# VectorE block turns and DRAM exchanges for latents, rotary keys and memory queries in a two-layer hybrid encoder

## The chip, the cores and the metric

The kernel runs on one core of a Trainium2 chip (trn2). TensorE (PE) multiplies matrices, VectorE (DVE) and ScalarE (ACT) work element by element, GpSimd (POOL) and SyncE (SP) mostly issue DMAs. The metric is the device time of one launch in microseconds, the median over runs.

## What is computed

```python
for l in range(2):
    h = rmsnorm(x, pre_norm_g[l]);  z = h @ w_in[l]               # 512 tokens, 2048 wide
    q_lat, kv_lat, k_pe, gb, gc, xin, q_mem, gate = split_cols(z)
    q = rmsnorm(q_lat, q_norm_g[l]) @ w_uq[l]                     # 512 -> 8 heads x (128 + 64 rotary)
    k_nope, v = rmsnorm(kv_lat, kv_norm_g[l]) @ w_ukv[l]          # 256 -> 8 heads x (128 + 128)
    a_out = softmax attention of the 8 heads, k = [k_nope, rope(k_pe) shared]
    c_out = gb * conv3(gc * xin)
    m_out = attention of 4 heads (q_mem) over 256 memory tokens
    y = concat(a_out, c_out, m_out) * silu(gate)
    x = x + rmsnorm(y @ w_o[l], post_norm_g[l])
```

Everything is float32. A product is made of three TensorE matmuls: each operand is split into a high part (a cast to fp32r on ScalarE) and a low part (the rest, by VectorE), and high x high, high x low and low x high are added (`mm3`, lines 272 to 274; `split_to`, lines 277 and 278).

## The kernel before

**Weights.** A block of weights (128 x 1024, `wr`) comes by DMA, ScalarE casts the high half `wh` (L189), VectorE makes the low half `wl` (L190). TensorE runs 12 matmuls of 512 columns on such a block. A few blocks are in flight, so a cast waits until TensorE has left an older block. SP and POOL issue the loads in the order of the program.

**Projections.** Input and output projection use Strassen-Winograd products (P1 to P7) that are gathered in PSUM banks. The input projection has several groups of columns; the last one, "group 4", makes the gates `ga0` and `ga1` of the latent attention. Between its 28 blocks the kernel does what the attention needs: it normalises the latents (`normalise`, L983), rotates the shared key (`k_rope`), and turns both to columns.

**Turns.** Activations lie with tokens on partitions; attention needs features on partitions. In the kernel before, latents (`lat`: cq and ckv), memory queries (`qm`) and the rotary key (`krA`, `krB`) are turned by TensorE, four 128x128 transposes into a PSUM bank (`turn4`, L915, tile `tps`; `k_rope_turn`, L1021, tile `krps`), which ScalarE and VectorE then split into high and low parts. Gates go another way: VectorE turns 32x32 blocks in place (`blocks_turned`, L933), and 16 DMAs per slab of 64 KB each (`exchange`, L941) put the blocks where they belong, from SBUF to SBUF.

**Attention.** First come the rotary queries (`q_rope_steps`: `qr` on TensorE, five VectorE instructions L1067 to L1077 into `rm`, a cast `qrh`, then a trip through DRAM, `qrd` to `QR`), then four memory heads, then eight latent heads in pairs. Per head and block of 128 queries: scores `sc`, maximum `nm`, exponential `P` (L1185), scale by `rec`, turns of P into `ptp`, their split `PT`, output `o`. Queries, keys and values of the pair (`qps`, `kps`, `vps`) are computed between the memory heads, and copied out of PSUM into `Q`, `K`, `V` in two halves by ScalarE and VectorE. There are eight PSUM banks, of which each tile takes one; a tile waits for the reading of the bank's last occupant.

**Order.** Every engine runs its instructions in a fixed order that is settled when the program is built: the kernel writes steps (`put`, `add`, `defer`, `between`), and a scheduler merges them by the times that it expects. Whichever tile (a slab of 1 MB, a bank) is claimed earlier is served earlier.

**The end.** The last block of the output projection needs `T4h` and `T4l`, the split of combined weights. The residual is read back per tile of 128 tokens, in the last layer with four DMAs (`fetch`, L1372).

Of the kernel before, what the change touches and what calls it, by code (L numbers as in the profile page):

```python
# [5 lines left out]
F32 = mybir.dt.float32  # L6
# [55 lines left out]
BLOCKS = "gm", "ga0", "ga1"  # L62
# [165 lines left out]
def encoder(tc, x, xt, mem, memt, positions, columns, w_in, q_norm_g, w_uq, w_qr, kv_norm_g, w_ukv,  # L228
# [160 lines left out]
    def tables_turned():  # L389
        G["tabd"] = dram.tile([P, 2 * S], F32, name="tabd")  # L390
        for n, wide in enumerate(G.pop("wides")):
            ps = bank("tab")
            for t in range(NT):
                nc.tensor.transpose(ps[:, t * P:(t + 1) * P], wide[:, t * P:(t + 1) * P], G["ident"])
            tab = scrap("tab")
            nc.scalar.copy(tab, ps)
            nc.gpsimd.dma_start(G["tabd"][:, n * S:(n + 1) * S], tab)
# [3 lines left out]
    class Left:  # L401
# [8 lines left out]
        def split(self, name, p, src):  # L410
            t = self.ops[name, p] = slab(f"{name}{p}", F32R)
            if self.apart:
                hi, lo = (t[:, o:o + 1024].rearrange("p (t g j) -> p g t j", t=2, j=32) for o in (0, 1024))
                split_to(hi, lo, src.rearrange("p g (t j) -> p g t j", j=32))
                return
# [324 lines left out]
    def projection(l):  # L740
# [8 lines left out]
        def own(*names):  # L749
            def f():  # L750
                for n in names:
                    C[n] = slab(n).rearrange("p (g t j) -> p t g j" if n in BLOCKS else "p (t g j) -> p t g j", t=NT, j=32)
            return f
# [27 lines left out]
        def gated(*names):  # L781
            def fin(i, j, tt, ps=None):
                if names[j] is None:
                    return
                v = C[names[j]][:, 2 * i + tt]
                nc.scalar.activation(v, v if ps is None else ps, AF.Silu)

                def turn():
                    blocks_turned(v)
# [4 lines left out]
        fin_m, fin_a = gated("gm", None), gated("ga0", "ga1")  # L794
# [123 lines left out]
    def y_slab(k):  # L918
        if k not in G["ys"]:
            G["ys"][k] = slab("y").rearrange("p (j c) -> p j c", j=4)  # L920
        return G["ys"][k]
# [9 lines left out]
    def blocks_turned(v):  # L931

        nc.vector.transpose(v, v)  # L933

    def exchange(dst, src):


        for p in range(4):
            for b in range(4):
                a = src[32 * p:32 * p + 32].rearrange("i t (c b) j -> i c b (t j)", b=4)[:, :, b]  # L940
                nc.sync.dma_start(dst[32 * b:32 * b + 32, :, P * p:P * p + P], a)  # L941

    def gate_rows(k, name, C):
        def f():
            pr.until(lambda: C.get((name, "turned")) == NT)
            exchange(y_slab(k), C[name])
        return f

    def conv_turn(l, c, C):
        def f():  # L950
            ps = turn4(lambda t: C["gc"][:, t], c)
            y, w = y_slab(2)[:, c, :], G[f"cw{l}"]
# [7 lines left out]
            nc.vector.tensor_tensor(in_tiles(y), in_tiles(y), of_tiles(g), op=ALU.mult)  # L960
        return f

    def qm_turn(j, C):
        def f():
            if j == 0:
                G["Qm"] = tuple(slab(n, F32R).rearrange("p (i c) -> p i c", i=4) for n in ("QmH", "QmL"))
            ps = turn4(lambda t: C["qm"][:, t], j)
            hi, lo = G["Qm"][0][:, j, :], G["Qm"][1][:, j, :]
            nc.scalar.activation(hi, ps, AF.Copy, scale=SC_MEM)
            nc.vector.scalar_tensor_tensor(lo, ps, SC_MEM, hi.bitcast(F32), op0=ALU.mult, op1=ALU.subtract)  # L970
        return f

    def normalise(views, n, gain, by=None):
# [8 lines left out]
        def times(t, v):  # L982
            return lambda: nc.vector.scalar_tensor_tensor(v, v, r[:, t:t + 1], gain, op0=ALU.mult, op1=ALU.mult)  # L983
# [7 lines left out]

    def latents_begin(l, C):
        G["q"] = [v[:, :QR_] for v in C["lat"]]
        G["kv"] = [v[:, O_KV:O_KV + KVR] for v in C["lat"]]
        normalise(G["q"], QR_, G["grow"][0], SC_MLA)
        normalise(G["kv"], KVR, G["grow"][1])
        pr.defer(0.0, lambda: G.update(normalised=l))

    def k_rope(C):
# [7 lines left out]
        nc.vector.tensor_tensor(m1, m1, m2, op=ALU.add)  # L1007
        kr = m1.rearrange("p t s i -> p t (s i)")
        krA = scrap("krA", dt=F32R).rearrange("p (t d i) -> p t d i", t=NT, d=2)
        krB = scrap("krB", dt=F32R).rearrange("p (t d i) -> p t d i", t=NT, d=2)  # L1010
        for d in range(2):
            nc.scalar.copy(krA[:, :, d, :], kr)
            nc.vector.tensor_tensor(krB[:, :, d, :], kr, krA[:, :, d, :].bitcast(F32), op=ALU.subtract)
        G["kr"] = krA, krB

    def k_rope_turn():
        kab = slab("KAB", F32R)
        for n, src in enumerate(G["kr"]):
            ps = bank("krps", F32R)
            for t in range(NT):  # L1020
                nc.tensor.transpose(ps[:, t * P:(t + 1) * P], src[:, t].rearrange("p d i -> p (d i)"), G["identr"])  # L1021
            nc.scalar.copy(kab[:, n * S:(n + 1) * S], ps.bitcast(F32))
        G["KA"], G["KB"] = kab[:, :S], kab[:, S:2 * S]

    def latent_turn(l, tag, j):
        def f():
            if j == 0:
                pr.until(lambda: G.get("normalised") == l)
                if tag == "cq":
                    G["cq"] = tuple(slab(n, F32R).rearrange("p (k c) -> p k c", c=S) for n in ("cqH", "cqL"))  # L1030
                else:
                    both = slab("ckv", F32R).rearrange("p (s k c) -> p s k c", s=2, k=2)
                    G["ckv"] = both[:, 0], both[:, 1]
            views = G["q" if tag == "cq" else "kv"]
            ps = turn4(lambda t: views[t], j)
            H, L = G[tag]
            split_to(H[:, j, :], L[:, j, :], ps)
        return f


# [7 lines left out]
    def q_rope_steps(l, g):  # L1048
        st = {}

        def products(n):
            def f(*ops):
# [7 lines left out]
                for k in range(4):  # L1060
                    mm3(ps, (hi[:, k, n], lo[:, k, n]), (cH[:, k, :], cL[:, k, :]), k == 0, k == 3)
# [34 lines left out]
    def qkv_steps(l, pair, st):  # L1096
# [9 lines left out]
        def fq(i):  # L1106
            def g(*ch):
# [6 lines left out]
                for j in range(4):  # L1114
                    mm3(ps, (hi[:, j, :], lo[:, j, :]), (cH[:, j, :], cL[:, j, :]), j == 0, j == 3)
# [3 lines left out]
        def fk(i):  # L1119
            def g(*ch):  # L1120
# [6 lines left out]
                for j in range(2):  # L1127
                    mm3(ps, (hi[:, j, i * 256:i * 256 + P], lo[:, j, i * 256:i * 256 + P]),
                        (cH[:, j, :], cL[:, j, :]), j == 0, j == 1)
# [3 lines left out]
        def fv(b):  # L1133
            def g():
# [5 lines left out]
                for i in range(2):  # L1140
                    sl = slice((2 * b + i) * P, (2 * b + i + 1) * P)
                    for j in range(2):
                        mm3(ps[:, i * 256:(i + 1) * 256].rearrange("p (h c) -> p h c", h=2),
                            (cH[:, j, sl], cL[:, j, sl]), (hi[:, j], lo[:, j]), j == 0, j == 1)
# [6 lines left out]
    def head_iters(j, rope, src, keys, whole=False):  # L1151
# [19 lines left out]
        def score(t):  # L1171
            def g():
# [3 lines left out]
                mm3(ps, (QH[:, sl], QL[:, sl]), (KH, KL), True, rope is None)  # L1176
                if rope is not None:
                    q = G["QR"][rope // 4][:, rope % 4, sl]
                    nc.tensor.matmul(ps, q, G["KA"], start=False, stop=False)  # L1179
                    nc.tensor.matmul(ps, q, G["KB"], start=False, stop=True)  # L1180
# [21 lines left out]
        def av(b):  # L1202
            def g():
# [7 lines left out]
                if b == 1:  # L1211
                    y = G["ys"][j // 4][:, j % 4, :]
                    nc.vector.tensor_tensor(in_tiles(y), of_tiles(st["o"]), in_tiles(y), op=ALU.mult)
# [4 lines left out]
    def mla_head(h, st):  # L1218
        i = h % 2

        def src():
            Q, K, V = st["Q"], st["K"], st["V"]
            ds = slice(i * P, (i + 1) * P)
            return (Q[:, 0, i], Q[:, 1, i], K[:, 0, i], K[:, 1, i]), (lambda k: V[:, 0, k, ds], lambda k: V[:, 1, k, ds])
        return head_iters(h, h, src, S, h < HEADS - 1)

    def mem_head(i):
        def src():
            Q, K, V = G["Qm"], G["Km"], G["Vm"]
            ds = slice(i * P, (i + 1) * P)  # L1230
            return ((Q[0][:, i], Q[1][:, i], K[:, 0, i], K[:, 1, i]),
# [30 lines left out]
    def mixer(l, C, pair2, tail):  # L1262
# [3 lines left out]
        put(p0, rotate0)  # L1266
# [415 lines left out]
```

## Time and profile before

| | |
|---|---|
| median of 3 runs | 1473.79 us (1472.41 to 1474.55) |
| profiled execution | 1472.93 us, span from first to last instruction 1471.2 us |
| granted TensorE clock | 0.997 |
| PE, DVE, ACT, POOL busy | 99%, 75%, 59%, 19% |
| moved by DMA | 295.22 MB, 201 GB/s |
| group 4 of layer 0, first query matmul after it | from about 351 us; 432.24 us |

A row of a timeline is: start, duration, engine, source line, instruction, output <- input, shapes, count; in brackets the idle time before it and who ended it. In rows of groups the idle time stands at the end. A row that begins with two times and a colon is a window.

### The profile page before, as it was taken

To read this page: it belongs to the slowest core of one execution; us is meant where nothing else is said; L and a number is where in the kernel's file an instruction comes from. 1 tells how busy PE (TensorE), PEld (TensorE's weight loads), DVE (VectorE), ACT (ScalarE), POOL (GpSimd) and SP (SyncE) were. 2 spreads that over 40 slices of the span, in tenths; PEclk is the share of its full clock that TensorE was granted. 3 is DMA by queue.
4 is the path that set the end of the run, shared out by engine and by line. 5 is a ranking of instruction groups with operands and counts; after the bars stand their busy time and mean duration, and the time that the engine had idled before them with its cause. 6 is when DMAs were issued, how large, how long until landed. Compare 5 with 4: busy or idle time off the path is not lost.

```text
span 1471.2 us, 19483 instructions
## 1 busy us (share of the span) xinstructions
PE 1454.2 (99%) x7104; PEld 1239.1 (84%) x7104; DVE 1096.7 (75%) x1461; ACT 870.4 (59%) x1328; POOL 275.2 (19%) x288
## 2 busy tenths in 40 slices
PE   9999999999999999999999999999999999999996
PEld 8888888899888888888898888888988888888885
DVE  5899677957677778868879665776576777778786
ACT  7856345446458688644777434454465687775543
POOL 0032302032301100311210333020322100003021
PEclk9999999999999999999999999999999999999998
DMA  9999979697967382795987999796979655139864
GB/s 358 402 272 228 216 187 190 168 188 221 220 217 180 79 265 87 137 250 143 329 290 230 241 237 223 188 179 161 212 196 248 201 140 115 44 87 170 244 128 158
DMA packets 156672, 295.22 MB, mean 201 GB/s; under 512 B 11616, under 2 KB 46944, under 8 KB 152736
## 3 DMA queue, kind: packets, MB, share of 16 engines
q0 software_dynamic: 56768, 129.52, 43.8%
q1 hardware_dynamic: 99808, 164.45, 35.1%
q8 instruction: 56, 0.92, 0.3%
q14 instruction: 40, 0.33, 0.1%
HBM read 266.01 MB, written 21.63 MB: 196 GB/s over the span
## 4 chain that ended last, share of the span: by engine, by line
PE 88%; DMA 4%; DVE 4%; ACT 2%; issue 1%; SPq 0%; POOL 0%; POOLq 0%; DVEq 0%; ACTq 0%
PE P L273 22%; PE P L274 22%; PE P L272 22%; DMA wr<-in_w_in_dram 2%; PE ptp L1198 2%; PE o L273 1%; PE o L274 1%; PE o L272 1%; PE sc L272 1%; DVE wl L190 1%; PE sc L274 1%; PE sc L273 1%; PE tps L915 1%; PE sc L1179 1%; PE qps L272 1%
## 5 line engine op out<-in xcount | busy, mean ns | idle before, releaser
L189 ACT CAST wh<-wr 128x1024 fp32r<-128x1024 f32 (+2 forms) x436 | 445.0, 1023 | 443.0 <-PE P L274 340.2
L190 DVE TENSOR_TENSOR wl<-wr,wh 128x1024 fp32r<-128x1024 f32 (+2 forms) x436 | 515.9, 1186 | 255.2 <-ACT wh L189 251.7
L272 PE MATMUL P<-wh,S 128*128 128x512 f32 (+1 forms) x896 | 345.1, 385 | 0.0
L273 PE MATMUL P<-wl,S 128*128 128x512 f32 (+1 forms) x896 | 343.7, 384 | 0.0
L274 PE MATMUL P<-wh,S 128*128 128x512 f32 (+1 forms) x896 | 343.2, 383 | 0.0
L272 PE MATMUL P<-wh,A 128*128 128x512 f32 (+1 forms) x656 | 253.0, 386 | 0.0
L273 PE MATMUL P<-wl,A 128*128 128x512 f32 (+1 forms) x656 | 251.8, 384 | 0.6 <-DVE wl L190 0.6
L274 PE MATMUL P<-wh,A 128*128 128x512 f32 (+1 forms) x656 | 251.5, 383 | 0.0
L146 POOL DMA_DIRECT2D wr<-in_w_in_dram x132 | 158.3, 1199 | 443.6 <-DVE wl L190 279.8
L274 PEld LDWEIGHTS P<-wh,S 128*128 128x128 f32 x896 | 168.2, 188 | 30.3
L272 PEld LDWEIGHTS P<-wh,S 128*128 128x128 f32 x896 | 168.1, 188 | 29.9
L273 PEld LDWEIGHTS P<-wl,S 128*128 128x128 f32 x896 | 168.2, 188 | 29.4
L273 PEld LDWEIGHTS P<-wl,A 128*128 128x128 f32 x656 | 123.2, 188 | 22.9 <-DVE wl L190 1.4
L274 PEld LDWEIGHTS P<-wh,A 128*128 128x128 f32 x656 | 123.1, 188 | 22.2
L272 PEld LDWEIGHTS P<-wh,A 128*128 128x128 f32 x656 | 123.1, 188 | 21.8 <-ACT og L586 0.2
L146 POOL DMA_DIRECT2D wr<-in_w_o_dram x40 | 48.6, 1248 | 295.1 <-DVE wl L190 291.2
L1185 ACT ACTIVATE P<-sc,nm 128x512 f32<-128x512 f32 (+1 forms) x96 | 59.8, 623 | 28.7 <-DVE nm L1182 28.4
L1182 DVE TENSOR_REDUCE nm<-sc 128x1 f32<-128x512 f32 (+1 forms) x96 | 56.8, 595 | 14.3 <-PE sc L1180 9.1
L1188 ACT ACTIVATE P<-P,rec 128x512 f32<-128x512 f32 (+1 forms) x96 | 61.7, 659 | 8.0 <-DVE rec L1187 8.0
L1198 PE MATMUL ptp<-identr,P 128*128 128x128 f32 x320 | 46.2, 273 | 2.3 <-ACT P L1188 2.3
L178 DVE TENSOR_TENSOR wr<-wr,wr 128x1024 f32<-128x1024 f32 (+1 forms) x36 | 42.2, 1175 | 4.5 <-DMA wr<-in_w_in_dram 4.1
L1198 PEld LDWEIGHTS ptp<-identr,P 128*128 128x128 f32 x320 | 38.0, 140 | 8.8 <-ACT P L1188 3.0
(318 smaller groups left out, 2082.6 us busy)
## 6 DMA issues: line engine op xcount, KB each, us to landing
wr<-in_w_in_dram SPq DMA_DIRECT2D x128, 512.0 KB, 5.2
wr<-in_w_in_dram POOLq DMA_DIRECT2D x108, 512.0 KB, 7.4
wr<-in_w_o_dram SPq DMA_DIRECT2D x48, 512.0 KB, 6.6
wr<-in_w_o_dram POOLq DMA_DIRECT2D x40, 512.0 KB, 7.1
wr<-in_w_in_dram SPq DMA_DIRECT2D x32, 416.0 KB, 3.7
wr<-in_w_in_dram POOLq DMA_DIRECT2D x24, 416.0 KB, 5.9
wr<-in_w_mk_dram SPq DMA_DIRECT2D x15, 512.0 KB, 8.7
wr<-in_w_mv_dram SPq DMA_DIRECT2D x15, 512.0 KB, 10.6
```

Source lines behind the costliest of these rows:

```text
L146: engine.dma_start(dst, src, **kw)
L178: nc.vector.tensor_tensor(tiles[a], tiles[a], tiles[b], op=ALU.add)
L189: pin(nc.scalar.copy(hi[:, h], src[:, h]))
L190: pin(nc.vector.tensor_tensor(lo[:, h], src[:, h], hi[:, h].bitcast(F32), op=ALU.subtract))
L272: nc.tensor.matmul(ps, ah, bh, start=first, stop=False, **kw)
L273: nc.tensor.matmul(ps, ah, bl, start=False, stop=False, **kw)
L274: nc.tensor.matmul(ps, al, bh, start=False, stop=last, **kw)
L915: nc.tensor.transpose(ps[:, t * P:(t + 1) * P], v[:, 4 * j:4 * j + 4].rearrange("p g j -> p (g j)") if len(v.shape) == 3 else v[:, j * P:( ...
L1182: nc.vector.tensor_reduce(nmax, ps, axis=AX.X, op=ALU.max, negate=True)
L1185: nc.scalar.activation(pt, ps, AF.Exp, bias=nmax, accum_out=tot)
L1188: nc.scalar.activation(pt, pt, AF.Copy, scale=rec)
L1198: nc.tensor.transpose(ps[:, k * P:(k + 1) * P], pt[:, k * P:(k + 1) * P], G["ident"])
```

## The change

1. Memory queries, normalised q and kv latents and the rotated key are turned by VectorE in 32x32 blocks, as the gates are, in slabs `ql` (two instructions), `kvl` (one; it holds kv latents and key) and `qm`. The 48 turns per layer on TensorE go. Weight columns are put in block order beforehand.
2. The blocks are exchanged through DRAM: one send per slab (two for `kvl`) with `sent`, then four fetches in runs of 2 KB with `fetched`. The gates, which had 16 DMAs per slab, use the same way. The high and low parts of the latents are made from the fetched slab in SBUF (`latents_parts`, `qm_parts`), in instructions of 1024 or 768 columns.
3. Operands keep the block layout (`spots`, `by_tokens`): matmuls read runs of 128 tokens. Operands of the output projection in layer 0 are split in two instructions instead of one.
4. The residual in the last layer is fetched with one DMA per tile instead of four.
5. Sends and fetches stand at new places among the steps.

```diff
-    def blocks_turned(v):
-        nc.vector.transpose(v, v)
-    def exchange(dst, src):
-        for p in range(4):
-            for b in range(4):
-                a = src[32 * p:32 * p + 32].rearrange("i t (c b) j -> i c b (t j)", b=4)[:, :, b]
-                nc.sync.dma_start(dst[32 * b:32 * b + 32, :, P * p:P * p + P], a)
+    def sent(key, *parts):
+        n = sum(t.shape[-1] for t in parts) // 4
+        d = G["sent", key] = dram.tile([4, P, n], F32, name=nm(f"sent{key}"))
+        o = 0
+        for t in parts:
+            w = t.shape[-1] // 4
+            nc.sync.dma_start(d[:, :, o:o + w].rearrange("b q k -> q b k"), t.rearrange("q (b k) -> q b k", b=4))
+            o += w
+    def fetched(key, name, c=4):
+        t, d = slab(name), G.pop(("sent", key))
+        for b in range(4):
+            nc.sync.dma_start(t[32 * b:32 * b + 32, :512 * c].rearrange("i (p k) -> i p k", p=4),
+                              d[b].rearrange("(p i) k -> i p k", p=4))
+        return t
...
+    def latents_parts():
+        t, hi = G.pop("cqw"), slab("cqH", F32R)
+        lo = t.bitcast(F32R)
+        for h in (slice(0, 1024), slice(1024, D)):
+            pr.defer(1.2, lambda h=h: split_to(hi[:, h], lo[:, h], t[:, h]))
...
-        put(p0, rotate0)
+        put(p0)
+        add(sent_rows("ga1", C))
+        put(rotate0)
...
-        between.setdefault(2, []).append((gate_rows(0, "ga0", C), []))
+        between.setdefault(2, []).append((sent_rows("ga0", C), []))
+        between.setdefault(4, []).append((gate_back(0, "ga0"), []))
         between.setdefault(6, []).append((fetch0, []))
-        between.setdefault(12, []).append((gate_rows(1, "ga1", C), []))
+        between.setdefault(9, []).append((gate_back(1, "ga1"), []))
...
-                if last:
-                    for i in range(NT):
-                        nc.gpsimd.dma_start(x[32 * i:32 * i + 32], G["src"][P * i + 32 * t:P * i + 32 * t + 32, :])
-                else:
-                    nc.gpsimd.dma_start(x, G["src"][t * P:(t + 1) * P, :])
+                nc.gpsimd.dma_start(x, G["src"].rearrange("(t p j) c -> p t j c", p=4, j=32)[t] if last else
+                                    G["src"][t * P:(t + 1) * P, :])
...
-        put(g4[8:13])
-        add(gate_rows(3, "gm", C))
-        put(g4[13:16])
-        lat = [latent_turn(l, "cq", j) for j in range(4)] + [latent_turn(l, "ckv", j) for j in range(2)] + [k_rope_turn]
-        more = [(f, []) for f in lat + [qm_turn(j, C) for j in range(4)]]
-        put(weave(g4[16:], more, 2, 2)[:-2])
+        put(g4[8:14])
+        add(lambda l=l: latents_sent(l))
+        put(g4[14:17])
+        add(latents_back)
+        add(lambda: G.update(qmw=fetched("qm", "QmL")))
+        put(g4[17:20])
+        add(latents_parts)
+        add(qm_parts)
+        put(g4[20:24])
+        add(gate_back(3, "gm"))
```

The order of TensorE's matmuls stays as it was, without the turns. On the other engines instructions move, at three places above all.

VectorE in group 4, where the products of ga1's first half are read out of their banks (`P`), before:

```order
L190 TENSOR_TENSOR wl_3456<-wr_3162,wh_3455 128x1024
L278 TENSOR_TENSOR cqL_3440<-tps_3441,cqH_3439 128x512
L278 TENSOR_TENSOR cqL_3440<-tps_3448,cqH_3439 128x512
L543 TENSOR_TENSOR ga_128_3030<-ga_127_3029,P_131_3041 128x16x32
L543 TENSOR_TENSOR ga_128_3030<-ga_127_3029,P_132_3042 128x16x32
L190 TENSOR_TENSOR wl_3474<-wr_3200,wh_3473 128x1024
```

and after:

```order
L190 TENSOR_TENSOR wl_3455<-wr_3176,wh_3454 128x1024
L190 TENSOR_TENSOR wl_3473<-wr_3214,wh_3472 128x1024
L190 TENSOR_TENSOR wl_3500<-wr_3267,wh_3499 128x1024
L547 TENSOR_TENSOR ga_134_3042<-ga_133_3041,P_137_3053 128x16x32
L547 TENSOR_TENSOR ga_134_3042<-ga_133_3041,P_138_3054 128x16x32
```

The two readings of P moved behind two more weight splits (wr_3200 and wr_3214 are the same block).

ScalarE in the memory heads, where the values V leave their first bank, before:

```order
L277 CAST PT_3962<-ptp_4014 128x2x128
L1188 ACTIVATE P_3974<-P_3974,rec_3977 128x256
L1185 ACTIVATE P_4008,tot_4009<-sc_4002,nm_4006 128x256
L277 CAST V_4031<-vps_4032 128x512
L1188 ACTIVATE P_4008<-P_4008,rec_4011 128x256
L1185 ACTIVATE P_4025,tot_4026<-sc_4019,nm_4023 128x256
```

and after:

```order
L1207 ACTIVATE P_4098,tot_4099<-sc_4092,nm_4096 128x256
L1210 ACTIVATE P_4098<-P_4098,rec_4101 128x256
L189 CAST wh_4106<-wr_3590 128x1024
L189 CAST wh_4110<-wr_3610 128x1024
L277 CAST V_3975<-vps_3976 128x512
```

Before, it was the eleventh exponential that stood ahead of V; now it is the sixteenth and last (P_4098) with two weight casts. The casts of K and the VectorE rotation `rm` moved back in the same way, and in the last latent heads of a layer the second pair of `PTl` on VectorE stands behind the split of an operand S, which stood behind it.

ScalarE at the end of the kernel, around T4h, before:

```order
L189 CAST wh_12764<-B_1184_12445 128x1024
L586 COPY og_11668<-P_1182_12415 128x512
L1346 ACTIVATE junk,ssqo_1123_11669<-og_11668 128x512
L586 COPY og_11679<-P_1183_12416 128x512
L189 CAST T4h_12768<-wr_12256 128x1024
L189 CAST T4h_12768<-wr_12274 128x1024
```

and after:

```order
L189 CAST wh_12634<-B_1180_12327 128x1024
L189 CAST T4h_12638<-wr_12138 128x1024
L189 CAST T4h_12638<-wr_12156 128x1024
L189 CAST T4h_12658<-wr_12174 128x1024
L189 CAST T4h_12658<-wr_12192 128x1024
L590 COPY og_11550<-P_1178_12297 128x512
```

The four casts moved ahead of the copies of the products.

More of the change, by code (lines that the diff above doesn't have):

```diff
@@ L61 @@
 RAW, PIECES, SLABS = 8, 4, 19
[L62 removed]
+BLOCKS = "gm", "qm", "ga0", "ga1"
 class Unit:
@@ L412, in split @@
             if self.apart:
[L413 to L414 removed]
+                if src.shape[-1] == P:
+                    split_to(t[:, :1024], t[:, 1024:], src.rearrange("q g k -> q (g k)"))
+                    return
+                hi, lo = (t[:, o:o + 1024].rearrange("q (t c p j) -> q t p c j", t=2, p=4, j=32) for o in (0, 1024))
+                for i in range(2):
+                    split_to(hi[:, i], lo[:, i], src[:, :, 32 * i:32 * i + 32].rearrange("q (p c) j -> q p c j", p=4))
                 return
@@ L916, in turn4, with spots, by_tokens @@
         return ps
[L918 to L921, printed above, removed]
+    def spots(t, c=4):
+        return t.rearrange("q (p c k) -> q c p k", p=4, c=c)
+    def by_tokens(a):
+        return a.rearrange("q (p k) -> q p k", p=4)
     def of_tiles(a):
@@ L1006, in k_rope @@
                 nc.vector.tensor_tensor(m2[:, t, s, :], kp[:, 1 - s, :], G["sin2"][:, t, s, :], op=ALU.mult)
[L1007 to L1030, printed above, removed]
-                else:
[L1032 to L1038, printed above, removed]
+        kr = G["kvl"][:, 1024:1536].rearrange("p (g t j) -> p t g j", t=NT, j=32)
@@ new lines, in k_rope, with latents_sent @@
+        nc.vector.tensor_tensor(kr[:, :, :2], m1, m2, op=ALU.add)
+        nc.scalar.copy(kr[:, :, 2:], kr[:, :, :2])
+        for h in (slice(0, 1024), slice(1024, D)):
+            pr.defer(1.2, lambda h=h: nc.vector.transpose(G["ql"][:, h], G["ql"][:, h]))
+        pr.defer(1.8, lambda: nc.vector.transpose(G["kvl"][:, :1536], G["kvl"][:, :1536]))
+        pr.defer(0.0, lambda: G.update(normalised=l))
+    def latents_sent(l):
+        pr.until(lambda: G.get("normalised") == l)
+        sent("ql", G.pop("ql"))
+        kv = G.pop("kvl")
+        sent("kvl", kv[:, :1024], kv[:, 1024:1536])
@@ new lines, in latents_back, with there @@
+    def latents_back():
+        G["cqw"], G["ckw"] = fetched("ql", "cqL"), fetched("kvl", "ckvL", 3)
+    def latents_parts():
+        t, hi = G.pop("cqw"), slab("cqH", F32R)
+        lo = t.bitcast(F32R)
+        for h in (slice(0, 1024), slice(1024, D)):
+            pr.defer(1.2, lambda h=h: split_to(hi[:, h], lo[:, h], t[:, h]))
+        kt, khi = G.pop("ckw"), slab("ckvH", F32R)
+        klo = kt.bitcast(F32R)
+        for h in (slice(0, 768), slice(768, 1536)):
+            pr.defer(1.0, lambda h=h: split_to(khi[:, h], klo[:, h], kt[:, h]))
+        def there():
+            G["cq"] = spots(hi), spots(lo)
+            kh, kl = (spots(a[:, :1536], 3) for a in (khi, klo))
+            G["ckv"] = kh[:, :2], kl[:, :2]
+            G["KA"], G["KB"] = kh[:, 2], kl[:, 2]
+            G["latents"] = True
+        pr.defer(0.0, there)
@@ L1470, in use @@
             G["ys"] = {}
+            for n in ("cq", "ckv", "Qm"):
+                G.pop(n, None)
         ms = mem_steps(l)
@@ L1589, in encoder @@
         put(g4[2:8])
-        add(lambda C=C: k_rope(C))
-        put(g4[8:13])
-        add(gate_rows(3, "gm", C))
-        put(g4[13:16])
-        lat = [latent_turn(l, "cq", j) for j in range(4)] + [latent_turn(l, "ckv", j) for j in range(2)] + [k_rope_turn]
-        more = [(f, []) for f in lat + [qm_turn(j, C) for j in range(4)]]
-        put(weave(g4[16:], more, 2, 2)[:-2])
+        add(lambda l=l, C=C: k_rope(l, C))
+        put(g4[8:14])
[8 more added lines that the diff above has]
+        add(gate_back(3, "gm"))
+        put(g4[24:26])
         add(mem_fetch)
-        put(weave(g4[16:], more, 2, 2)[-2:])
-        G["left"] = Y = Left(False, l + 1 < depth)
+        put(g4[26:])
+        add(lambda: pr.until(lambda: "Qm" in G and "cq" in G))
+        G["left"] = Y = Left(False, True)
         g0, g1, gains, fetch = out_proj(l)
```

106 lines of the change are left out of this document (59 added, 47 removed).

## The prediction

> **What bounds the kernel now.** I read the page's busy shares, then the waits of TensorE (us in all, times, longest), then the timelines of the stages that the change touches:
>
> ```profile
> PE 1454.2 (99%) x7104; PEld 1239.1 (84%) x7104; DVE 1096.7 (75%) x1461; ACT 870.4 (59%) x1328; POOL 275.2 (19%) x288
> ...
> PE ptp L1198 <- ACT P L1188: 2.3, 2, 1.1
> ...
> 432.24 0.48 PE L272 MATMUL qr<-cqH,wh 128*128 128x512 f32 x1
> 433.02 0.39 PE L272 MATMUL qr<-cqH,wh 128*128 128x512 f32 x1
> 437.56 0.39 PE L274 MATMUL qr<-cqH,wl 128*128 128x512 f32 x1
> ```
>
> TensorE is nearly never idle, so whatever leaves its queue is time won, and every new pause of it is time lost. Its largest wait inside the layers is 1.1 us for one late probability, once a layer. Matmuls of 512 columns start 0.227 us apart (20 of them from 433.02 to 437.56), a weight block of 12 takes 2.7.
>
> All sums stand against the profiled execution, 1472.93 us (span 1471.2). The median, 1473.79, lies 0.86 above it; I add that at the end.
>
> **The turns that leave TensorE.** The instructions (duration, count, both layers), and two places in the chain of work that ended last (krB's eight turns read like krA's):
>
> ```profile
> L915 PE MATMUL tps<-identr,lat x48: 270/272/273, 399.9 to 1139.4; 128*128 128x128 f32 x48
> L915 PE MATMUL tps<-identr,qm x32: 272/272/297, 419.6 to 1158.3; 128*128 128x128 f32 x32
> L1021 PE MATMUL krps<-identr,krA x8: 223/240/251, 418.9 to 1145.2; 128*128 128x128 f32 x8
> ...
> 400.08 0.87 PE tps L915 x8
> 419.08 0.64 PE krps L1021 x8
> ```
>
> They are pipelined: eight take 0.87 on the path, 0.109 each, not 0.27; a key turn 0.08. 80 x 0.109 + 16 x 0.08 = -10.0 us, all of it on the path. The matmuls that use the turned operands stay as many; they read them in runs of 128 instead of 512 tokens, which I cost at nothing.
>
> **The turns that VectorE gets**, in the last group of the input projection (latents done, gates being made):
>
> ```profile
> L933 DVE STREAM_TRANSPOSE ga<-ga 128x512 f32<-128x512 f32 x7 | 4.8, 700 | 0.2 <-ACT ga L786 0.2
> ...
> 340.00:371.00 31.00, 31.00 (x148) 27.41 (x147) 25.97 (x41) 20.52 (x38) 7.93 (x10) 1.00 0.73 196
> ...
> 369.98 0.75 DVE L1013 TENSOR_TENSOR krB<-kpm,krA 128x256 fp32r<-128x256 f32 x2
> 371.32 1.23 DVE L190 TENSOR_TENSOR wl<-wr,wh 128x1024 fp32r<-128x1024 f32 x1 [0.59 <-ACT wh L189]
> 374.05 1.22 DVE L190 TENSOR_TENSOR wl<-wr,wh 128x1024 fp32r<-128x1024 f32 x1 [1.50 <-ACT wh L189]
> ```
>
> Two of 1024 and one of 1536 columns, 0.7 per 512: some 4.7 us, less 0.8 for the key's low halves that go. They fall where VectorE has just caught up (it first idles at 371.32, then 1.5 per block). Ends: 0, all inside the lead of the low weight halves, and 3.9, none; with one or two blocks of lead I take 1.5 a layer, +3.0. The memory queries' turns fall in the group before, on VectorE too; their two sends stand ahead of four weight loads on SP's queue: 0 to 2 us, taken as 0.
>
> [...]
>
> **The round trip through DRAM.** Before, nothing waited for it; now the split latents do:
>
> ```profile
> 378.39 19.74 SPq L941 DMA_DIRECT2D y<-gm  x16
> 401.07 1.07 ACT L277 CAST cqH<-tps 128x512 fp32r<-128x512 f32 x2
> ...
> QR<-qrd POOLq DMA_DIRECT2D x16, 256.0 KB, 7.1
> ...
> Vmd<-Vm POOLq DMA_DIRECT2D x2, 1024.0 KB, 8.3
> ...
> qrd<-rm POOLq DMA_DIRECT2D x4, 512.0 KB, 5.5
> ```
>
> SP is done with the weight loads at 378.4. A 1 MB send lands some 8 us after, 388; the fetches, four issues each, land by about 399 to 403. The new cast of cq stands at about 403.5 on ScalarE: nothing to pay, margin 1 to 5 us. If it is gone, casts and splits of weights queue behind the late cast and TensorE stops 1:1. The gates' fetches are needed only by the latent heads, over 20 us later. The rotated queries, which already go through DRAM (the rows of QR and qrd), start that trip 14 us later by place 2 below, at t 24: 5.5, four issues, 7.1 make 39, needed at 41; 0, with a margin of 2. The residual's single DMA per tile lands as one instead of four; nothing waits for it, 0.
>
> **Three places where the static order holds TensorE.** In order, per layer:
>
> (1) The last group's product banks. Before, VectorE emptied them right after two splits of cq; now after two more weight splits:
>
> ```profile
> 402.34 1.28 DVE L278 TENSOR_TENSOR cqL<-tps,cqH 128x512 fp32r<-128x512 f32 x2
> 403.54 1.27 DVE L543 TENSOR_TENSOR ga<-ga,P 128x512 f32<-128x512 f32 x2
> 403.72 1.05 ACT L189 CAST wh<-wr 128x1024 fp32r<-128x1024 f32 x1 [1.59 <-PE P L274]
> ```
>
> The last of those splits needs a cast that ScalarE can only start when TensorE has left the block before (the 1.59 wait). So TensorE comes to the banks, and then run: 0.2 release, cast 1.05, split 1.15, emptying 0.68: 3.2 idle a layer, +6.4.
>
> (2) The memory heads (first query matmul at 432.24 = t 0):
>
> ```profile
> 445.97 0.44 PE L1198 MATMUL ptp<-identr,P 128*128 128x128 f32 x2 [1.13 <-ACT P L1188]
> 461.77 0.36 PE L272 MATMUL sc<-Km,QmH 128*128 128x256 f32 x1
> 465.10 0.48 PE L272 MATMUL sc<-K,Q 128*128 128x512 f32 x1
> ...
> 435.45 1.23 DVE L1067 TENSOR_TENSOR rm<-qr,tab 128x1024 f32<-128x1024 f32 x1
> 451.42 0.68 DVE L278 TENSOR_TENSOR K<-kps,K 128x512 fp32r<-128x512 f32 x1
> 457.63 0.68 DVE L278 TENSOR_TENSOR V<-vps,V 128x512 fp32r<-128x512 f32 x1
> ...
> 441.19 1.05 ACT L277 CAST qrh<-rm 128x1024 fp32r<-128x1024 f32 x1
> 465.67 1.99 ACT L189 CAST wh<-wr 128x1024 fp32r<-128x1024 f32 x2
> ```
>
> Before: the rotation (five instructions, 3.6 us, from 435.45) ahead of the softmax, K after the sixth exponential, V after the eleventh. Now the rotation stands after the fourth PT split, K in a block with four PT casts after the twelfth exponential, V after the sixteenth and two weight casts. I walked the new order by hand with the durations of these rows. Softmax starts earlier (first turn of P at t 12.4, was 13.7, its 1.13 pause gone). Then VectorE rotates from t 17.4 to 21.4, ScalarE waits 1.9 for it; the K block, VectorE's 0.7 at its end, frees the bank of the 13th score at 28.4, 3.5 later than before; the last memory score comes at 33.7 (was 29.5). V: last scale ends 36.0, two weight casts 2.0, V cast 0.5, and on VectorE both low halves to 39.5, V 0.7: first latent score at 40.2, where it was 32.9. With 0.3 at the output behind it 7.7; in layer 1 one scale stands ahead of the second K cast, 8.5: +16.2.
>
> (3) The last latent heads, where out-projection operands are split between them:
>
> ```profile
> 582.32 1.27 DVE L278 TENSOR_TENSOR PTl<-ptp,PTh 128x512 fp32r<-128x512 f32 x2
> 583.46 0.39 PE L272 MATMUL o<-PTh,V 128*128 128x512 f32 x1
> 584.29 1.23 DVE L278 TENSOR_TENSOR S<-y,S 128x1024 fp32r<-128x1024 f32 x1
> ```
>
> The second pair of PTl now follows two maxima, the first pair and two half splits of S: six instructions of 0.6 behind a probability, 3.3 after the output needs them, and 1.0 at the score ahead: about 4.1 a layer, +8.2.
>
> **The tail gains.** ScalarE's T4h casts now precede the copies that waited for the last products:
>
> ```profile
> 1443.95 0.59 ACT L586 COPY og<-P 128x512 f32<-128x512 f32 x1 [5.75 <-PE P L274]
> 1446.39 3.88 ACT L189 CAST T4h<-wr 128x1024 fp32r<-128x1024 f32 x4
> 1447.49 0.80 PE L272 MATMUL P<-T4h,A 128*128 128x512 f32 x1 [2.22 <-ACT T4h L189]
> 1449.73 0.80 PE L273 MATMUL P<-T4l,A 128*128 128x512 f32 x1 [1.45 <-DVE T4l L190]
> 1462.30 0.39 PE L274 MATMUL P<-T4h,A 128*128 128x512 f32 x1
> 1447.20:1454.10 6.90, 5.17 (x11) 3.76 (x12) 6.90 (x7) 3.07 (x4) 0.00 (x0) 0.51 0.21 83
> ```
>
> (The last row is a window: span, busy time and count of each engine, granted clock, DMA share and GB/s.) Casts done by about 1442 and low halves by 1445 let T4's 48 matmuls start at 1445.1 and end at 1456.0 instead of 1462.5: pauses 3.7 and half clock gone, -6.7.
>
> **The clock.** That row shows that a pause of 2.2 us is followed by granted clock 0.5; the 1.13 pause at 445.97 was not. The new order has six pauses of about 3 us (place 1, before the first latent score, place 3, twice). After the second pause there the slow stretch was 4.4 us, 2.2 lost; ends 0 and 2.2 each; I take 1.0, +6: these pauses are longer than the one that did it, but stand alone, where the tail has two in a row.
>
> **Sum.** 1472.93 - 10.0 + 3.0 + 6.4 + 16.2 + 8.2 - 6.7 + 6 = 1496.0, and 0.9 to the median: 1496.9. My walk counts every wait in full; engines a little ahead of it make it less, so I say 1495.
>
> **The rivals.**
> - *The waits don't bind (faster).* The order is the same, but TensorE has other banks and work in hand when one is late. Then only -10.0, -6.7 and +3.0 count: 1460. It decides if places 1 to 3 cost under 14 us in all instead of 31. For it: in the old order all such waits came to 1.1 us a layer. Against: TensorE's queue is in order, and that 1.1 was one probability late by as much. 0.14.
> - *One or two of the places cost nothing,* by slack that I don't see: 1472 to 1487. 0.16, a quarter of it within 0.2%.
> - *The clock stays full:* 1491. For it: the 1.13 pause passed. Against: the tail. 0.18.
> - *The clock falls at all six pauses, 2.2 each:* 1504. For it: the tail's row, with a shorter pause. 0.08. [...]
> - *The round trip is late* past its margin, 3 to 5 us a layer: above 1504. 0.05.
>
> **How the numbers follow.** My forecast, places and clock as counted, 1491 to 1501, has 0.39. A measurement of this kernel can tell 0.2% (2.9 us) from no change. Faster: the first rival, 0.14. Same: the quarter of the second, 0.04. Slower: the rest, 0.82. Without the first rival and the late round trip (0.19) the cases reach from about 1472 to 1504: that is the range.
>
> **What would show it.** Right: no turns of lat and qm on TensorE; TensorE idle 3 us each time at the second pass of the last group, at the first score from K, and at the last output of a layer; no wait for T4h at the end. Wrong: those waits under 1 us, or a DMA named ahead of cq's cast on ScalarE. What would make the forecast wrong is above all place 2, half of the loss.

## The result, and the profile after

The changed kernel takes 1535.01 us (median of 4, 1524.37 to 1538.15), the kernel before in the same runs 1473.57: a ratio of 1.0405, interval 1.0378 to 1.0431. Five further runs of it gave 1531.98 (1.0403, 1.0385 to 1.0422). I had said 1495, with 1472 to 1504 as the range. The direction was right, the forecast loss about a third of the measured one.

The profiled execution took 1538.15 (span 1536.3, granted clock 0.979). First its busy line from the page, then the waits of TensorE (us in all, times, longest):

```profile
PE 1465.4 (95%) x7008; PEld 1241.2 (81%) x7008; DVE 1108.2 (72%) x1477; ACT 873.2 (57%) x1328; POOL 270.4 (18%) x276
```

```profile
PE P L272 <- DVE ga L547: 13.6, 2, 6.8
PE P L272 <- ACT wh L189: 11.5, 2, 6.3
PE o L273 <- DVE PTl L278: 6.1, 2, 3.1
PE sc L272 <- DVE V L278: 5.4, 2, 2.7
PE P L273 <- DVE wl L190: 5.3, 6, 1.3
```

Third and fourth row are places 3 and 2 of the forecast, each near the 3 us of idle time that it named (3.1 and 2.7). The first is place 1, but 6.8 long instead of 3.2, and the second wasn't in the forecast at all. Both are in group 4. For T4h TensorE waits no more, as forecast. The timeline of ScalarE and TensorE there, in layer 0, says who is late:

```profile
410.79 1.04 ACT L189 CAST wh<-wr 128x1024 fp32r<-128x1024 f32 x1 [5.36 <-DMA wr<-in_w_in_dram]
415.32 1.99 ACT L277 CAST cqH<-cqL 128x1024 fp32r<-128x1024 f32 x2 [3.48 <-DMA cqL<-sentql]
426.20 0.83 ACT L277 CAST ckvH<-ckvL 128x768 fp32r<-128x768 f32 x1 [8.89 <-DMA ckvL<-sentkvl]
...
413.84 0.77 PE L272 MATMUL P<-wh,S 128*128 128x512 f32 x1 [6.78 <-DVE ga L547]
429.07 0.80 PE L272 MATMUL P<-wh,S 128*128 128x512 f32 x1 [5.19 <-ACT wh L189]
```

Each of the two pauses of TensorE ends behind a ScalarE cast that waited for a DMA: the first behind a weight load 5.36 late, the second behind the fetch of ckv 8.89 late. The weight cast behind that one in ScalarE's queue (427.99) is what TensorE then waits for. The cast of cq in the second row waited 3.48 too; that is the sign of being wrong that the prediction had named, a DMA ahead of cq's cast. The DMA rows (KB each, median us from issue to landing) show the trip, and the same two kinds of transfer for the gates:

```profile
sentql<-ql SPq DMA_DIRECT2D x2, 1024.0 KB, 14.9
cqL<-sentql SPq DMA_DIRECT2D x8, 256.0 KB, 17.2
ckvL<-sentkvl SPq DMA_DIRECT2D x8, 192.0 KB, 15.7
sentkvl<-kvl SPq DMA_DIRECT2D x2, 512.0 KB, 21.0
sentkvl<-kvl SPq DMA_DIRECT2D x2, 256.0 KB, 26.6
...
sentga<-ga SPq DMA_DIRECT2D x4, 1024.0 KB, 6.3
y<-sentga SPq DMA_DIRECT2D x16, 256.0 KB, 9.9
```

The same 1 MB send takes 6.3 in the attention and 14.9 in group 4, and the two sends of kvl, issued right behind, take 21.0 and 26.6. A warning stood in the trace of before (first two windows, of its group 4: span, busy times, clock, DMA share, GB/s):

```profile
380.00:390.00 10.00, 10.00 (x46) 8.29 (x45) 6.66 (x8) 5.94 (x8) 4.34 (x4) 1.00 1.10 230
390.00:400.00 10.00, 10.00 (x46) 8.23 (x45) 4.90 (x4) 3.49 (x4) 3.41 (x4) 1.00 1.12 205
62.80:72.50 9.70, 9.70 (x47) 7.95 (x45) 5.89 (x10) 7.17 (x10) 2.03 (x3) 1.00 1.02 412
786.80:793.80 7.00, 7.00 (x32) 5.79 (x32) 5.87 (x10) 5.06 (x8) 1.07 (x2) 1.00 0.97 330
```

The DMA engines were already full in group 4 (share above 1.0). TensorE waited for none of them there, so it cost nothing; the change put such a wait in. But the share by itself would not have given the price. The last two rows are the times of the two `Vmd` sends, from whose median of 8.3 the prediction took its 8 us: they landed in 9.7 and 7.0 at a share of about 1 as well.

For all comparisons I cut each profiled execution at marks of TensorE's timeline, each the start of a matmul, and add the two layers: group 4 (last matmul of 416 columns to first query product `qr`), memory heads (to the first latent score from `K,Q`), latent heads (to the last `o` made from `PTh`), and the end (first T4 matmul to the end of the span). All in us:

| kernel | group 4 | memory heads | latent heads | end | span |
|---|---|---|---|---|---|
| before | 163.0 | 65.8 | 241.8 | 23.7 | 1471.2 |
| changed | 190.4 | 84.0 | 259.1 | 24.9 | 1536.3 |
| changed, again | 183.4 | 82.5 | 259.6 | 24.1 | 1529.7 |
| resid4 | 172.7 | 83.7 | 260.6 | 23.8 | 1518.4 |
| b_resid1 | 163.0 | 65.6 | 241.8 | 27.1 | 1474.1 |
| no_trip | 154.9 | 69.2 | 251.4 | 25.9 | 1481.7 |
| no_accum | 165.5 | 83.9 | 259.2 | 21.8 | 1506.5 |
| act_send | 175.2 | 78.1 | 262.6 | 26.1 | 1520.4 |
| tab24 | 175.8 | 74.6 | 253.3 | 24.6 | 1508.8 |
| stack | 173.4 | 74.8 | 242.1 | 19.4 | 1486.2 |
| lat_pe | 159.6 | 75.1 | 243.7 | 19.3 | 1475.0 |
| lat_t24 | 159.6 | 76.5 | 241.6 | 19.9 | 1475.2 |
| b_sp4 | 163.0 | 65.7 | 241.8 | 19.5 | 1464.9 |

The change's 65.1 us of span are 27.4 in group 4, 18.2 and 17.3 in the heads, 1.2 at the end, and 1.0 elsewhere. Group 4 of the changed kernel differs by up to 18 us between executions with the same order up to there (190.4, 183.4, and 172.7 in resid4); in the three executions of the kernel before in the table (before, b_resid1, b_sp4) it is 163.0 each time.

### The profile page after: what moved, and what is told of

Same layout as the page of the kernel before. It is cut to its first block, busy times and chain, and to the rows that moved or that the text cites. A ratio compares the mean times of both kernels' runs of the same rounds, so it can differ in the third digit from the quotient of the medians.

```text
span 1536.3 us, 19277 instructions
## 1 busy us (share of the span) xinstructions
PE 1465.4 (95%) x7008; PEld 1241.2 (81%) x7008; DVE 1108.2 (72%) x1477; ACT 873.2 (57%) x1328; POOL 270.4 (18%) x276
## 3 DMA queue, kind: packets, MB, share of 16 engines
q0 software_dynamic: 58112, 129.52, 41.5%
## 4 chain that ended last, share of the span: by engine, by line
PE 74%; DMA 12%; DVE 6%; issue 4%; ACT 2%; POOL 1%; SPq 1%; POOLq 0%; DVEq 0%; ACTq 0%
PE P L273 18%; PE P L274 17%; PE P L272 17%; DMA sentkvl<-kvl 3%; DVE wl L190 2%; DMA wr<-in_w_in_dram 2%; PE ptp L1220 2%; DMA ckvL<-sentkvl 2%; DMA xr<-xs 1%; PE o L273 1%; PE o L274 1%; PE o L272 1%; PE sc L272 1%; PE sc L274 1%; PE sc L273 1%
## 5 line engine op out<-in xcount | busy, mean ns | idle before, releaser
L273 PE MATMUL P<-wl,S 128*128 128x512 f32 (+1 forms) x896 | 347.2, 387 | 5.1 <-DVE wl L190 5.1
L272 PEld LDWEIGHTS P<-wh,S 128*128 128x128 f32 x896 | 169.9, 190 | 57.6 <-issue 14.4
L274 PEld LDWEIGHTS P<-wh,S 128*128 128x128 f32 x896 | 169.9, 190 | 30.6
L273 PEld LDWEIGHTS P<-wl,A 128*128 128x128 f32 x656 | 123.3, 188 | 22.8 <-DVE wl L190 1.2
```

What stands on the lines that cost most here:

```text
L272: nc.tensor.matmul(ps, ah, bh, start=first, stop=False, **kw)
L273: nc.tensor.matmul(ps, ah, bl, start=False, stop=False, **kw)
L274: nc.tensor.matmul(ps, al, bh, start=False, stop=last, **kw)
```

## Experiments

**The trip taken out (no_trip).** Rivals: the late trip, or the casts and splits that now stand between those of the weights.

```diff
-        sent("ql", G.pop("ql"))
-        kv = G.pop("kvl")
-        sent("kvl", kv[:, :1024], kv[:, 1024:1536])
...
-        G["cqw"], G["ckw"] = fetched("ql", "cqL"), fetched("kvl", "ckvL", 3)
+        G["cqw"], G["ckw"] = G.pop("ql"), G.pop("kvl")
```

> The changed kernel without the trip of latents and rotary key through DRAM: no sends and fetches of ql and kvl, the parts are made straight from the turned slabs, so blocks aren't exchanged and the attention works on wrongly placed tokens. Theory (the trip and the weight loads that it delays on saturated DMA engines stop TensorE in group 4): the two pauses there shrink to the 3 us of the bank emptying, some 14 us a layer, 28 in all with the half clock behind them: 1505 to 1510. Rival (the casts and splits that stand between those of the weights are the cause, whatever they wait for): 6 us less at most, 1529 or more.

Measured: 1485.22 (1482.08 to 1488.68), 1.0078 of before (1.0058 to 1.0099): 50 us less, more than the theory said. Group 4 falls to 154.9, which is 8.1 below before: nearly the whole 10.0 of the turns is there, so VectorE's turns and place 1 cost at most 1.9 in this order. But place 1 itself is another: without the trip VectorE empties the banks after one weight split fewer, at 402.83, and TensorE doesn't pause there. The memory heads fell too (69.2), because the scheduler starts the rotation ahead of the first maximum again. So this run changes the trip and places 1 and 2 together, and no_accum and tab24 separate them.

**The jam (no_accum).** By the jam I mean that many transfers share full DMA engines and each lands late. Here the order of instructions is the same on every engine, and only the weight loads are lighter (GpSimd's queue takes 28.2% of the 16 engines' span instead of 41.5%).

```diff
-            move(nc.gpsimd, tiles[u.key], 0, u.more, accum_op=ALU.add)
+            move(nc.gpsimd, tiles[u.key], 0, u.more)
```

> The changed kernel with the second half of each paired weight load written plainly instead of added in the DMA (it leaves out that sum, so the weights are others); the order of instructions on every engine is the same. Theory (the DMA engines are jammed in group 4, most of all by these adding loads, whose 2 KB packets take some 0.2 us against 0.09 for plain ones, and the trip of the latents shares them): sends and fetches land in 7 to 11 us instead of 15 to 21, group 4 takes 79 to 83 us a layer instead of 94 to 96, in all 24 to 32 us less: 1503 to 1511. Rival (the trip is slow by its own form, runs of 2 KB and their issue): 5 us less at most.

Measured: 1508.81 (1506.07 to 1514.04), 1.0238 (1.0220 to 1.0257). Its DMA rows:

```profile
sentql<-ql SPq DMA_DIRECT2D x2, 1024.0 KB, 9.6
cqL<-sentql SPq DMA_DIRECT2D x8, 256.0 KB, 9.5
...
sentkvl<-kvl SPq DMA_DIRECT2D x2, 512.0 KB, 10.2
```

Sends and the fetch of cq land in some 10 us, near what I had counted on, and group 4 falls by 24.9, to 165.5; the heads do not move (83.9 and 259.2 against 84.0 and 259.1). So the jam costs 24.9 of the first execution's group 4, 17.9 of the second's (183.4), and 23 to 26 by the medians. The DMA share from 380 to 430 is still 1.02 to 1.15, against 1.08 to 1.15 in the changed kernel, so the share doesn't tell the two runs apart. ScalarE still waited 5.2 for ckv in layer 0, where TensorE no longer paused behind it. What is left in group 4 is place 1, but for one wait of 1.5 in layer 1 (the last row is a window, with the granted clock after the busy times):

```profile
406.88 1.28 DVE L547 TENSOR_TENSOR ga<-ga,P 128x512 f32<-128x512 f32 x2
...
407.71 0.76 PE L272 MATMUL P<-wh,S 128*128 128x512 f32 x1 [3.08 <-ACT cqH L277]
408.27 0.63 PE L273 MATMUL P<-wl,S 128*128 128x512 f32 x1
408.70 0.63 PE L274 MATMUL P<-wh,S 128*128 128x512 f32 x1
...
413.39 0.41 PE L273 MATMUL P<-wl,S 128*128 128x512 f32 x1
413.64 0.39 PE L274 MATMUL P<-wh,S 128*128 128x512 f32 x1
...
407.70:413.40 5.70, 5.69 (x14) 4.44 (x15) 2.79 (x4) 0.57 (x1) 0.00 (x0) 0.50 1.24 333
```

3.08 against the 3.2 of my walk. (The releaser named, the cast of cq, is the event nearest in time; in the changed kernel the same matmul started at 413.84, before that cast began at 415.32. The first half of the emptying by VectorE, in the first row, ends at about 407.6.) Then the matmuls start 0.43 apart instead of 0.227, at a granted clock of 0.50: 14 steps in 5.93 instead of 3.18, so the half clock costs another 2.75 a pause. Twice 5.8 is 11.7, and no_trip, where place 1 is gone as well, has a group 4 that is 10.6 shorter than this one: that leaves next to nothing for the trip itself with the lighter loads.

**Earlier sends (act_send).**

```diff
-        sent("ql", G.pop("ql"))
+        sent("ql", G.pop("ql"), by=nc.scalar)
...
-        sent("kvl", kv[:, :1024], kv[:, 1024:1536])
+        sent("kvl", kv[:, :1024], kv[:, 1024:1536], by=nc.scalar)
```

> The changed kernel with the sends of latents and rotary key issued by ScalarE instead of SyncE, so that they leave when the turns are done (372 and 376 us) and not when SyncE is through with its weight loads (380 to 384). Theory A (what counts is when the sends leave): the trip ends 6 to 7 us earlier, and group 4 loses that much a layer, 10 to 14 us in all: 1521 to 1525. Theory B (it is the jam that counts, and an earlier start only stands longer in it, while ScalarE pays for the issues): within 5 us of 1533.

Measured: 1519.94 (1516.65 to 1522.16), 1.0308 (1.0293 to 1.0323), 1 us below the range of theory A. The sends leave at 372.9 and 376.9 and 377.7, the fetch of cq is issued at 381.95 instead of 394.29. Group 4 is 15 shorter than in the first execution of the changed kernel, 8 than in the second, but 2.5 longer than in resid4. The run doesn't show theory A's cause, though: the edit moved VectorE's order too. It now empties the banks of place 1 one weight split earlier (at 404.82), and the pause there is gone, which was worth up to 11.7 in no_accum. How much of the gain is the earlier start and how much is place 1 stays open. The trip still isn't covered: fetches of 16.6, and waits of up to 4.5.

**Place 2 (tab24).** The scheduler had put the rotation late because its table arrives through a weight buffer that is claimed late.

```diff
         put(g4[24:26])
+        add(tables_fetch)
...
-        add(tables_fetch)
         (p0, rotate0, fetch0), (p1, rotate1, fetch1) = (q_rope_steps(l, g) for g in range(2))
```

> The changed kernel with the fetch of the rotation tables four weight blocks earlier, before the last two of group 4: it moves the five rotation instructions of VectorE back ahead of the first softmax maximum, as they stood in the kernel before. Theory (place 2 of the forecast: rotation, K and V late by the static order cost 8.8 and 9.5 us between first query product and first latent score): 14 to 18 us less, 1517 to 1521. Rival (that stretch is long because of half clock and of DMAs that run late out of group 4, not by the place of the rotation): 5 us less at most, 1530 or more.

Measured: 1509.43 (1507.55 to 1510.59), 1.0241 (1.0226 to 1.0256), 26 less. The stretch of the theory, the memory heads, is 9.4 shorter, so of its 18.2 about half; the latent heads are 5.8 shorter; the rest lies in group 4, which scatters by as much, and can't be credited to the table. The total lies below the theory's 1517 to 1521 because it holds these two as well. Where the first latent score waited 2.7 for V, nothing waits, but a new pause has come:

```profile
487.82 0.50 PE L272 MATMUL sc<-K,Q 128*128 128x512 f32 x1 [2.73 <-DVE V L278]
```

```profile
PE ptp L1220 <- ACT P L1210: 7.0, 2, 3.5
PE o L273 <- DVE PTl L278: 6.1, 2, 3.1
```

The first row is from the changed kernel, the other two are waits of tab24: the first probability is now 3.5 late in each layer, since VectorE rotates before it takes the maxima. Half of place 2 is thus traded, not won.

**The residual (resid4, b_resid1, after_again, b_sp4, b_sp1).** In resid4 the changed kernel gets the old four DMAs back, in b_resid1 the kernel before gets the single one (its diff is shown; that of resid4 is the reverse):

```diff
-                    for i in range(NT):
-                        nc.gpsimd.dma_start(x[32 * i:32 * i + 32], G["src"][P * i + 32 * t:P * i + 32 * t + 32, :])
+                nc.gpsimd.dma_start(x, G["src"].rearrange("(t p j) c -> p t j c", p=4, j=32)[t] if last else
+                                    G["src"][t * P:(t + 1) * P, :])
```

> The changed kernel with the residual of the last layer fetched by four DMAs of 32 tokens per tile again, nothing else. Theory (the single DMA of 1 MB is slow, 22.8 us, and holds back the last weight load behind it on GpSimd's queue and the last residual add): about 7 us less, 1528, with T4h waiting for no DMA and the end 9 us after the last matmul instead of 14. Rival (the whole end is late because of what comes before it, and the fetch only shares in that): within 1.5 us of the changed kernel's 1535.

> The kernel before with the residual of the last layer in one DMA per tile, nothing else. Theory (one DMA is itself slow): 5 to 8 us more than before, 1479 to 1482, since the last residual tile is then waited for. Rival (it is slow only beside the other transfers of the changed kernel, or nothing waits for it, as I forecast): within 1 us of 1473.6.

> The changed kernel once more, unaltered, as the measure of its own scatter: its first four runs lie between 1524 and 1538, those with only the residual fetch put back between 1520 and 1541, and the profiled executions differ in group 4 (94.2 and 96.2 against 85.4 and 87.3). Theory (arrival times on jammed DMA engines differ from run to run): again a spread of over 10 us and a median between 1524 and 1536, which leaves the residual fetch worth under 3 us. Rival (the residual fetch is worth the 9 us between the two medians): 1533 to 1537, spread under 8.

resid4: 1526.26, 1520.18 to 1540.7, 1.0389 (1.0333 to 1.0445). after_again: 1531.98, 1531.21 to 1538.6: the median that the theory named, but a spread of 7 and not of over 10. The medians differ by 6 to 9, but the end by only 1.1 (24.9 to 23.8), so the rest is group 4's scatter; by totals alone this pair decides nothing. b_resid1: 1474.39, ratio 1.0000 (0.9991 to 1.0010): its rival. But "nothing waits" isn't why. In b_resid1 the T4h casts move ahead and T4 takes 10.6 instead of 14.8; from the last T4 matmul to the end it takes 16.5 instead of 8.9, with this wait of VectorE and this landing:

```profile
DVE xr L1396 <- DMA xr<-xs: 8.5, 1, 8.5
```

```profile
xr<-xs POOLq DMA_DIRECT2D x4, 1024.0 KB, 23.2
```

A gain and a loss of the same edit cancel. Before, 256 KB landed in 7.9. In the changed kernel the slow DMA shows as follows (GpSimd, ScalarE, VectorE):

```profile
1502.56 1.22 POOL L146 DMA_DIRECT2D wr<-in_w_o_dram  x1 [17.24 <-DVE ms L282]
```

```profile
1509.82 1.06 ACT L189 CAST T4h<-wr 128x1024 fp32r<-128x1024 f32 x1 [4.53 <-DMA wr<-in_w_o_dram]
```

```profile
1526.26 1.28 DVE L1422 SCALAR_TENSOR_TENSOR xr<-og,r,xr 128x1024 f32<-128x1024 f32 x1 [6.69 <-DMA xr<-xs]
```

GpSimd idles 17 us between the residual's DMA and its last weight load. (The releaser named there is only the event nearest in time; the load does not wait for `ms` in the program. What held it, the records don't show. The load issued before it, at 1483.37 between two residual DMAs, landed only 20.7 later.) So the last T4h cast is 4.5 late, and the last residual add 6.7. Keeping the early casts without the slow DMA is one edit, in the kernel before:

```diff
-                        nc.gpsimd.dma_start(x[32 * i:32 * i + 32], G["src"][P * i + 32 * t:P * i + 32 * t + 32, :])
+                        nc.sync.dma_start(x[32 * i:32 * i + 32], G["src"][P * i + 32 * t:P * i + 32 * t + 32, :])
```

> The kernel before with the four DMAs of each residual tile issued by SyncE, which has nothing to do then, instead of GpSimd; it also puts the T4h casts of ScalarE ahead of the last product copies, as in the changed kernel. Theory (the early casts are worth the two pauses and the half clock in front of the last block, 4.3 us as the run with a single residual DMA showed, and that run gave it back because its transfer was late by as much): 4 to 6.5 us less than before, 1467 to 1470. Rival (the end waits for the residual or for VectorE whatever TensorE does): within 1 us of before.

Measured: 1467.20 (1465.85 to 1468.71), 0.9952 of before (0.9940 to 0.9965). It beats both kernels. T4 starts at 1445.49 without a pause, and 256 KB land in 5.0. From the last `o` to the first T4 matmul it takes 133.0 instead of 135.4, and the end 4.2 less: 6.6, where the forecast's tail said 6.7.

The single DMA by SyncE instead of GpSimd, in the kernel before:

> The kernel before with the residual in one DMA per tile, issued by SyncE. Theory A (a single DMA of four blocks of 32 rows keeps only half of the DMA engines busy, on any queue): it lands in 18 to 24 us, and the end waits for it, 1472 to 1476. [...]

Measured: 1487.05, one run, longer than theory A said; the trace gives no landing time for these DMAs. A window and a wait of it:

```profile
1430.00:1440.00 10.00, 7.71 (x20) 5.81 (x21) 6.64 (x6) 4.98 (x6) 0.62 (x1) 0.66 0.36 103
```

```profile
PE P L272 <- ACT wh L189: 8.9, 2, 5.5
```

Counted from the DMA records, mostly 3 or 4 packets of 8 KB are in flight here, for some 50 us (the DMA share is 0.25 to 0.27 of 16 engines from 1396 to 1410); in b_resid1 mostly 4 or 8 (4 while only its first tile is under way), and in b_sp4 mostly 16. The end is 19.7, shorter than before; the whole loss lies between the last `o` and the first T4 matmul, 149.9 instead of 135.4. The four weight loads that GpSimd issues beside the residual land in 13.4 to 14.0 instead of the 6.0 to 8.7 of b_sp4, ScalarE's T4h casts wait up to 9.1 for them, and the weight cast that TensorE waits for stands behind those casts. That these loads share the few busy engines fits the counts, but the records name no engine.

**Everything together (stack).** Edits of tab24, act_send and b_sp4, and, for place 3:

```diff
-        last_pair = {0: [(sums(0), []), g0[0][0]], 1: [g0[0][1]], 2: [g0[0][2]], 3: [g0[0][3]],
+        last_pair = {0: [g0[0][0]], 1: [g0[0][1]], 2: [(sums(0), []), g0[0][2]], 3: [g0[0][3]],
```

> The changed kernel with four edits together: tables fetched early (as above), sends of latents and key by ScalarE (as above), the sums for the output projection two steps later in the last pair of heads (so that the second pair of PTl no longer stands behind the splits of S, place 3 of the forecast), and the residual in four DMAs per tile by SyncE. Theory (the losses are separate and add up: about 25 for the tables' place, 13 for the sends, 10 to 12 for place 3, of which 3.1 a layer is the pause and 2 to 3 half clock, 6 for the end): 1478 to 1486, with no wait for PTl. Rival (the pauses stand in for one another: what is saved at one is waited for at the next): 1495 or more.

Measured: 1487.98 (1487.71 to 1489.46), 1.0101 (1.0086 to 1.0117), 2 us above the theory's range and far from the rival. The latent heads are back at 242.1, with no wait for PTl; against tab24 that is 11.2, 5.6 a layer, most of it place 3 with its half clock. In the changed kernel the place read:

```profile
612.07 0.80 PE L273 MATMUL o<-PTl,V 128*128 128x512 f32 x1 [3.08 <-DVE PTl L278]
612.66 0.63 PE L274 MATMUL o<-PTh,V 128*128 128x512 f32 x1
613.09 0.63 PE L272 MATMUL o<-PTh,V 128*128 128x512 f32 x1
```

What remains above before is 10.4 in group 4, where the trip has eaten the turns' gain as well (place 1's pause is gone here too, as in act_send, but TensorE still waits 9.2 for weight casts), and 9.0 in the memory heads.

**Latents by TensorE again (lat_pe, lat_t24).** Turns, splits and keys as before; memory queries and gates stay on the new way, the residual as in b_sp4. In these two the latents' tokens stand in their natural order while the other operands have block order, so the outputs are others; number and size of the latents' instructions are those of the kernel before. lat_t24 adds the edit for place 3 and the early tables.

> The changed kernel with latents and rotary key turned by TensorE and split from its banks as before, so that only memory queries and gates go through DRAM, and with the residual in four DMAs per tile by SyncE. Theory (all that the exchange costs outside place 3 comes from the trip of the latents): group 4 back at 81.5 or below, the stretch to the first latent score at 33 to 36, place 3 still there, the end 6 to 7 shorter: 1473.8 - 3.5 (turns of memory queries) + 10 (place 3) - 7 + 0 to 6 for the memory heads' order = 1473 to 1479. Rival (memory queries and gates through DRAM jam the engines as well): group 4 over 85 and 1485 or more.

> The same as the run before (latents and key by TensorE, residual by SyncE) with the sums of the output projection two steps later and the tables fetched early. Theory (place 3 and the heads' order are then gone and the turns of the memory queries are won): 1463 to 1468, at or below the 1467.2 of the kernel before with the residual by SyncE. Rival (gates and memory queries in 2 KB runs give nothing back, or another wait takes their place): 1470 or more.

lat_pe: 1476.72, 1.0025 (1.0016 to 1.0034), in the theory's range. Group 4 is at 159.6, 3.4 below before: that is the 32 turns of the memory queries (32 x 0.109 = 3.5), and gates and memory queries through DRAM cost nothing more there. The total is partly luck: I had expected place 3 to stay, and its order was gone already (243.7), while the memory heads are 9.3 longer than before instead of up to 6. lat_t24: 1474.81, 1.0011 (1.0002 to 1.0020), the rival. Its memory heads take 10.7 more than before:

```profile
PE ptp L1248 <- ACT P L1238: 8.9, 2, 4.5
```

```profile
439.78 1.22 DVE L1118 TENSOR_TENSOR rm<-qr,tab 128x1024 f32<-128x1024 f32 x1
```

The rotation begins 7.6 after the first query product (432.14; before, 3.2 after it), since it now stands behind the low half of one more weight block, and the first probability comes 4.5 late. Another wait has taken the place of the one removed.

## Why the forecast was wrong, point by point

- **Round trip at nothing: the step that failed.** I took 8 us for a 1 MB send from two sends of another stage, gave the sends of kvl no time of their own, and held a late trip at a chance of 0.05 and 3 to 5 us a layer. In group 4 the send of cq took 14.9 and those of kvl 21.0 and 26.6, beside the adding weight loads. That cost 24.9 us in the first execution, 17.9 in the second, as the run with the same order and lighter loads shows, and its scatter makes most of that of the kernel.
- **Residual at nothing: failed too.** The single DMA took 22.8 us, and VectorE waited 6.7 for it at the end. The tail's gain of 6.7 was real (6.6 in b_sp4), but the early casts and the slow transfer came from the same edit. At the end the changed kernel gained nothing: 0.3 less before T4 and 1.2 more after. Why one DMA keeps fewer packets of 8 KB in flight (mostly 4 or 8 in the changed kernel) than four (mostly 16 in the kernel before), no run shows.
- **Place 1: right.** 3.08 against 3.2.
- **Place 2: right in size.** The memory heads are 8.7 and 9.5 longer, against 7.7 and 8.5, with the wait for V at the first latent score that the walk gave. The rotated queries' trip, which I had put at 0 with a margin of 2, was late once: TensorE waited 1.6 for QR in layer 1, and 4.0 in resid4.
- **Place 3: right.** 3.08 and 0.66 a layer against 3.3 and 1.0, and with its edit in stack the wait is gone.
- **The clock: half of it.** I took 1.0 a pause from ends of 0 and 2.2. Behind the pauses of about 3 us it costs 2.75 (place 1) and 1.6 (place 3: eight steps in 3.42 instead of 1.82); the slow stretch behind the first latent score (matmuls 0.43 apart from 490.01 on) lies in the latent heads, which are 17.3 longer where I had 8.2 for place 3 and 2 for the clock.
- **Turns: right.** 10.0 off TensorE; the turns on VectorE at 1.9 or less in no_trip, against 3.0.

Added up against 1496.0: group 4 27.4 instead of 1.4 (turns, VectorE, place 1 and a third of the clock), heads 35.5 instead of 28.4, the end 0.9 instead of -6.7, elsewhere 1.3 instead of 0. That makes 42 more: 1538.

## What to carry to other kernels

Before a transfer is put on the path of the bound engine, read the DMA share of the stage in which it will run. If it is at 1, a landing time from another stage is no price: here 1 MB landed in 7 to 15 us at a share of about 1, and the send of cq scattered (14.9 and 13.1 in two executions of the changed kernel). What else the engines carry decided it here, the adding loads above all, so leave a margin of that size or keep the transfer off the path. Before DMAs are merged, look at the packets in flight, not at the count of DMAs: here four small ones with mostly 16 in flight landed in 7.9 us, one with 4 or 8 in 22.8. And where a scheduler sets the order, one edit moves others: price the order that it leaves, place by place, and test each edit alone before calling it free.

## What the hardware showed that I had not expected

- The weight loads that add in the DMA occupied the engines far longer here than the same loads written plainly. All loads of GpSimd's queue, for the same 129.52 MB, in the changed kernel and in no_accum:

```profile
q0 software_dynamic: 58112, 129.52, 41.5%
```

```profile
q0 software_dynamic: 35328, 129.52, 28.2%
```

  That is 0.415 x 1536.3 = 638 us of all 16 engines against 0.282 x 1506.5 = 425.
- One DMA of 1 MB took three times as long to land as each of four of 256 KB: 22.8 us in the changed kernel against 7.9 in the kernel before, with mostly 4 or 8 packets in flight instead of 16.
- A single pause of 3.08 us was followed by 8 slow matmul starts in one place and 14 in another, most of them 0.43 us apart instead of 0.227.
